# A two-layer streaming encoder step: the gated-linear-attention layer's near score products, and one attention in three, issued between the q and the k products of the next unit

## The chip, the cores and the metric

The kernel runs on one core of a Trainium2 chip. The metric is the device time of one execution in microseconds (us). Five engines each work through their own instructions in order: PE (TensorE: matrix products; its weight loads are shown as PEld), DVE (VectorE), ACT (ScalarE), POOL (GpSimd) and SP (which issues transfers). They wait for one another by semaphores.

## The reference, cut to what matters

The trunk has four blocks: retention, a convolutional feed-forward (FFN), gated linear attention (GLA), a second FFN. Only GLA is touched. Per head it computes, from projections q, k, v and a log gate lg:

```python
def gla_chunk(S, xs):
    q, k, v, lg = xs
    b = jnp.cumsum(lg, axis=1)
    expo = b[:, :, None] - b[:, None, :]          # -inf above the diagonal
    A = jnp.einsum('bihd,bjhd,bijhd->bhij', q, k, jnp.exp(expo))
    intra = jnp.einsum('bhij,bjhe->bihe', A, v)
    cross = jnp.einsum('bihd,bhde->bihe', q * jnp.exp(b), S)
    bL = b[:, -1]
    S_new = jnp.exp(bL)[..., None] * S + jnp.einsum('bjhd,bjhe->bhde', k * jnp.exp(bL[:, None] - b), v)
    return S_new, intra + cross
```

There are 4 heads, keys of 128, values of 256, 1024 prompt rows (one stream) and 32 rows of a running stream.

## The kernel before

GLA walks over 12 units `(h, c)`: head h, and c a third of the 1056 columns (384, 384, 288). A unit has three minor tiles of 128 rows; the third tile of c = 2 is the 32 sample rows. For each unit these steps are written out:

- `project`: `gate` (one product `pz`, on ACT the exponential and logarithm, on DVE the running sum `b`), then `qk_products`: 24 products for q (8 weight tiles, each in high x high, high x low, low x high parts, L133 to L135, tile `pj`) and 24 for k, and `qk_out`, which scales both into `q` (L1097) and `k` (L1099) on DVE.
- `weigh`: seven tiles `x64` to `x1` from `b`, one for each level of the score decomposition (differences on POOL, exponentials on ACT, products with k and q on DVE, L1150 and L1151, two a level), and `e`, `qh`, `ql`, `kd`, `eL`.
- `scores`: the near products into `pb` (diagonal 32x32 blocks L1199, level 16 L1202, levels 8, 4, 2, 1 L1208), then the far products of levels 64 and 32 into `pa` (L1215). They use 32 or 16 columns of the PE array each and are float32, so that each is two matmul records in the trace: 144 near and 24 far in a full unit. Then DVE masks `pb` into `A` (L1220, L1225), and ACT and DVE split `A` and `pa` into `Ah` and `Al` (L1247, L1248).
- `mix`: per minor tile `value` (24 products `pv`, L267 to L269, split into `vh` on ACT and `vl` on DVE) and `attend`: the state product `ouu` (L1338 to L1340), the new state `gS` on DVE (L1343), the output `ou` (L1354 to L1360), whose last product L1360 reads `gSl`, the low part of the state before, made on DVE (L1292) after its high part `gSh` on ACT (L1291). `keys` transposes `kd`; `late` transposes the unit before's output (`pt`, L1410).

The loop overlaps units by the order of the text: in the turn of unit u, the q and k products of the next unit come first, then `store[0]`, the third attention of the unit before u, then the scores of u, then its values and first two attentions. In a unit with c = 2 the third minor tile has no value products, so its second attention comes right after the first and the transposes. A scheduler keeps each engine's order near this text and moves some instructions by its own estimate; the PSUM tiles `pj`, `ou` and `lv` (which holds `pb`, `pa`, `pkt` and `pt`) have two buffers each.

Of the kernel before, what the change touches and what calls it, by code (L numbers as in the profile page):

```python
# [16 lines left out]
P = 128  # L17
# [3 lines left out]
TS = 32  # L21
# [17 lines left out]
def minors(c):  # L39
    c0, n = CM[c]  # L40
    out = []
    o = 0
    while o < n:
        ln = min(128, n - o)
        out.append((o, c0 + o, ln))
        o += ln
    return out
# [3 lines left out]
def trunk_kernel(ctx: ExitStack, tc: tile.TileContext, io):  # L51
    nc = tc.nc
    V, S, G, PE = nc.vector, nc.scalar, nc.gpsimd, nc.tensor
# [1012 lines left out]
    def gla(closers):  # L1066
# [10 lines left out]
        def groups_of(c):  # L1077
            return [(0, 3, P)] if c < 2 else [(0, 2, P), (2, 3, TS)]

        def qk_products(h, c, between=None):  # L1080
            c0, n = CM[c]
            if c == 0:

                wq[h] = weights("w_gqk", h, 0, after=(None, masked[0]))
                wk[h] = weights("w_gqk", h, 1, after=(None, masked[0]))
            pq = t384(pp, "pj", w=512)
            proj(pq[:, :n], wq[h], c0, n)
            if between:
                between()
            pk = t384(pp, "pj", w=512)  # L1090
            proj(pk[:, :n], wk[h], c0, n)
            return pq, pk

        def qk_out(c, ps):
            c0, n = CM[c]
            q = t384(g1, "q")
            V.tensor_tensor(q[:, :n], ps[0][:, :n], R[:, c0:c0 + n], op=ALU.mult)  # L1097
            k = t384(g1, "k")
            V.scalar_tensor_tensor(k[:, :n], ps[1][:, :n], float(GDK ** -0.5), R[:, c0:c0 + n],  # L1099
                                   op0=ALU.mult, op1=ALU.mult)  # L1100
            return q, k
# [14 lines left out]
            V.tensor_tensor_scan(b[:, :n], smask[:, :n], t2[:, :n], 0.0, op0=ALU.mult, op1=ALU.add)  # L1116
            return b

        def project(h, c):
            if (h, c) == (0, 1):  # L1120

                return None, *qk_out(c, qk_products(h, c))
            b = gate(h, c)
            return b, *qk_out(c, qk_products(h, c))

        def weigh(h, c, bqk):
            b, q, k = bqk
# [54 lines left out]
            V.tensor_tensor(kd[:, :n], kd[:, :n], k[:, :n], op=ALU.mult)  # L1182
            return q, k, X, qh, ql, kd, eL

        def scores(h, c, w):
            q, k, X, qh, ql, kd, eL = w
            mins = minors(c)
            groups = groups_of(c)

            full = [(mi, o) for mi, (o, t0, L) in enumerate(mins) if L == P]  # L1190
            F = len(full)

            pb = lv("pb")
            near = pb[:, :3 * TS].rearrange("p (m i) -> p m i", i=TS)
            low = pb[:, 3 * TS:9 * TS].rearrange("p (l m i) -> p l m i", l=4, i=TS // 2)
            for mi, (o, t0, L) in enumerate(mins):
                for a in range(0, L, TS):
                    b = o + a
                    PE.matmul(near[a:a + TS, mi], k[:, b:b + TS], q[:, b:b + TS], start=True, stop=True)  # L1199
                for a in range(0, L, TS):  # L1200
                    b = o + a
                    PE.matmul(near[a:a + TS // 2, mi, TS // 2:], X[16][:, b:b + TS // 2],  # L1202
                              X[16][:, b + TS // 2:b + TS], start=True, stop=True)
            for li, s in enumerate(LOW):
                for mi, (o, t0, L) in enumerate(mins):
                    for a in range(0, L, TS):
                        x = X[s][:, o + a:o + a + TS]
                        PE.matmul(low[a:a + TS, li, mi], x, x.rearrange("p (b t) -> p b t", t=2 * s)[:, :, s:],  # L1208
                                  start=True, stop=True)
            far = lv("pa").rearrange("p (m i) -> p m i", m=3)  # L1210
            for mi, o in full:
                for s, b in ((64, 0), (64, TS), (32, 2 * TS), (32, 0)):
                    c0 = 0 if s == 64 else 2 * TS
                    i0 = o + (2 * TS if s == 64 else b + TS)
                    PE.matmul(far[b:b + TS, mi, c0:c0 + s], X[s][:, o + b:o + b + TS], X[s][:, i0:i0 + s],  # L1215
                              start=True, stop=True)

            A = t384(g1, "A", bufs=1, w=3 * TS).rearrange("p (m i) -> p m i", i=TS)
            for m0, m1, L in groups:
                masked[0] = V.tensor_tensor(  # L1220
                    A[:L, m0:m1], near[:L, m0:m1], dmask[:L].unsqueeze(1).to_broadcast([L, m1 - m0, TS]), op=ALU.mult)
            for li, s in enumerate(LOW):
                for m0, m1, L in groups:
                    M, B = m1 - m0, TS // (2 * s)
                    masked[0] = V.copy_predicated(  # L1225
                        A[:L, m0:m1].rearrange("p m (b t) -> p m b t", t=2 * s)[:, :, :, s:],
                        lmask[:L, li].rearrange("p (b t) -> p b t", t=s).unsqueeze(1).to_broadcast([L, M, B, s]),
                        low[:L, li, m0:m1].rearrange("p m (b t) -> p m b t", t=s))
            if c == 1:
                second_mask[0] = masked[0]  # L1230
            whole[0] = masked[0]

            if len(tri) < 2:
                tri.append([t384(g2, f"{t}{len(tri)}", F32R, 1).rearrange("p (m i) -> p m i", i=P) for t in ("Ah", "Al")])
                for t in tri[-1]:
                    S.activation(t.rearrange("p m i -> p (m i)"), smask, AF.Copy, scale=0.0)
            else:
                tri.reverse()
            Ahv, Alv = tri[-1]
            khv, klv = [t384(g2, t, F32R, 2).rearrange("p (m i) -> p m i", i=P) for t in ("kh", "kl")]  # L1240
            As = g2.tile([P, TS], F32R, tag="As", name=f"As{uid()}", bufs=1) if F < 3 else None
            blocks = [(slice(a, a + TS), slice(a, a + TS), A[a:a + TS, :F]) for a in range(0, P, TS)]
            blocks += [(slice(0, 2 * TS), slice(2 * TS, P), far[:2 * TS, :F, :2 * TS])]
            blocks += [(slice(a, a + TS), slice(a + TS, a + 2 * TS), far[a:a + TS, :F, 2 * TS:3 * TS])
                       for a in (0, 2 * TS)]
            for rows, cols, src in blocks[4:] + blocks[:4]:
                S.copy(Ahv[rows, :F, cols], src)  # L1247
                order(V.tensor_tensor(Alv[rows, :F, cols], src, Ahv[rows, :F, cols].bitcast(F32), op=ALU.subtract),  # L1248
                      whole[0])
            if F < 3:  # L1250
                stack_left(As, A[:TS, F], 1.0)

            def keys():
                pkt = pp.tile([P, 3, P], F32, tag="lv", name=f"pkt{uid()}", bufs=2)
                for mi, (o, t0, L) in enumerate(mins):
                    PE.transpose(pkt[:L, mi], kd[:, o:o + L], ident)
                for m0, m1, L in groups:
                    if L == TS:
                        stack_left(khv[:, m0], pkt[:L, m0], 1.0)
                        continue  # L1260
                    cast[0] = S.copy(khv[:L, m0:m1], pkt[:L, m0:m1])
                    masked[0] = V.tensor_tensor(klv[:L, m0:m1], pkt[:L, m0:m1], khv[:L, m0:m1].bitcast(F32),
                                                op=ALU.subtract)
            return As, Ahv, Alv, qh, ql, khv, klv, eL, keys
# [3 lines left out]
        def mix(h, c, u, late, rows0):  # L1268
# [105 lines left out]
            if c == 0:  # L1374
# [2 lines left out]
                v = g2.tile([TS, GDV], F32, tag="vsum", name=f"vsum{uid()}")  # L1377
                vss[h] = g2.tile([P, GDV], F32R, tag="vhs", name=f"vhs{uid()}")
                stack_sample(vss[h], ps, v, GDV // 2, rc[:TS, 8:9])
            attend(1)  # L1380

            def finish():
                attend(2)
# [22 lines left out]
            def store(lv, room):  # L1406
                for e in range(2):
# [3 lines left out]
                    ot = room()  # L1411
                    S.copy(ot[:, :n], pt.rearrange("p m i -> p (m i)")[:, :n])
                    nc.sync.dma_start(scr_og[2 * h + e, :, c0:c0 + n], ot[:, :n])
            return finish, store, scaled, rows

        def lv(name):
            return pp.tile([P, 3, P], F32, tag="lv", name=f"{name}{uid()}", bufs=2).rearrange("p m t -> p (m t)")
# [30 lines left out]
        def between():  # L1448
            gates_out(0, g00)
            mid.append(mean(1))  # L1450
            early.append(gate(0, 0))
            early.append(gates_in(1))
# [16 lines left out]
        store = None  # L1469
# [3 lines left out]

        for i, u in enumerate(units):
            nxt = units[i + 1] if i + 1 < len(units) else None
            if nxt:
                p = project(*nxt)
            if store:
                store[0]()
            if nxt == (0, 1):  # L1480
                rms_b(2, lv("pr"))
                gates_out(2, gates_in(2))
            sc = scores(*u, w)
            if nxt == (0, 1):
                p = gate(*nxt), *p[1:]
            if store:
                store[2]()
            store = mix(*u, sc, late(store), store and store[3])
            if nxt:
                w = weigh(*nxt, p)  # L1490
# [1069 lines left out]
```

## Time and profile before

| what | value |
|---|---|
| device time, 3 runs | 2743.98 us median, 2743.62 to 2744.26 |
| profiled execution | 2745.33 us |
| its span, first to last instruction | 2743.6 us |
| PE busy | 2711.1 us, 99% of the span |
| DVE busy | 2052.2 us, 75% |
| ACT busy | 1384.6 us, 50% |
| POOL busy | 398.5 us, 15% |
| GLA units | from about 1573 to 1858 us of the span |

Busy times are sums over an engine's instructions. An idle stretch of an engine is shown before the instruction that ended it, with the instruction that released it; "issue" stands where the profile shows nothing that the engine waited for. In the lists of instructions, merged rows carry a count; the start of each row is counted from the span's start.

### The profile page before, as it was taken

To read this page: it belongs to the slowest core of one execution; us is meant where nothing else is said; L and a number is where in the kernel's file an instruction comes from. 1 tells how busy PE (TensorE), PEld (TensorE's weight loads), DVE (VectorE), ACT (ScalarE), POOL (GpSimd) and SP (SyncE) were. 2 spreads that over 40 slices of the span, in tenths; PEclk is the share of its full clock that TensorE was granted. 3 is DMA by queue.
4 is the path that set the end of the run, shared out by engine and by line. 5 is a ranking of instruction groups with operands and counts; after the bars stand their busy time and mean duration, and the time that the engine had idled before them with its cause. 6 is when DMAs were issued, how large, how long until landed. Compare 5 with 4: busy or idle time off the path is not lost. (4 is left out here: it accounts for less than half of the span.)

```text
span 2743.6 us, 55821 instructions
## 1 busy us (share of the span) xinstructions
PE 2711.1 (99%) x22416; PEld 2621.5 (96%) x22416; DVE 2052.2 (75%) x3648; ACT 1384.6 (50%) x2596; POOL 398.5 (15%) x671
## 2 busy tenths in 40 slices
PE   9999999999999999999999999999999999999998
PEld 8999987778999999999999999999999999999998
DVE  7876667776566988888876788875479888888666
ACT  7544355444445544444644467774355444445445
POOL 0000000000112211111211232220132111112113
PEclk9999999999999999999999999999999999999999
DMA  6233455554876244332988511116533433329884
GB/s 244 87 110 110 129 156 158 150 145 122 283 236 225 94 145 138 102 106 87 288 226 215 171 40 54 54 54 209 190 121 102 147 129 104 108 83 296 224 214 122
DMA packets 279444, 410.19 MB, mean 150 GB/s; under 512 B 57168, under 2 KB 209104, under 8 KB 275088
## 3 DMA queue, kind: packets, MB, share of 16 engines
q1 hardware_dynamic: 260384, 347.73, 39.1%
q0 software_dynamic: 18256, 58.35, 9.0%
q8 instruction: 175, 2.87, 0.5%
q14 instruction: 85, 0.70, 0.1%
q10 hardware_dynamic: 544, 0.54, 0.1%
HBM read 264.34 MB, written 142.21 MB: 148 GB/s over the span
## 5 line engine op out<-in xcount | busy, mean ns | idle before, releaser
L419 ACT COPY HR<-pu 128x264 f32<-128x264 f32 x264 | 98.6, 374 | 252.2 <-PE pu L445 246.1
L445 PE MATMUL pu<-XA,wgl 128*128 128x264 f32 x752 | 213.4, 284 | 0.0
L440 PE MATMUL pu<-XA,wgh 128*128 128x264 f32 x752 | 212.8, 283 | 0.4 <-ACT wgh L376 0.4
L444 PE MATMUL pu<-XA,wgh 128*128 128x264 f32 x752 | 212.5, 283 | 0.0
L2142 DVE SCALAR_TENSOR_TENSOR AR<-AR,cw 128x1058 f32<-128x1058 f32 x88 | 116.0, 1320 | 69.9 <-ACT AR L2141 59.2
L2115 DVE TENSOR_TENSOR AR<-HR,pu 128x264 f32<-128x264 f32 (+2 forms) x440 | 144.4, 370 | 4.2 <-ACT HR L419 2.8
L440 PEld LDWEIGHTS pu<-XA,wgh 128*128 128x128 f32 x752 | 141.2, 188 | 0.6 <-ACT wgh L376 0.6
L444 PEld LDWEIGHTS pu<-XA,wgh 128*128 128x128 f32 x752 | 141.2, 188 | 0.0
L445 PEld LDWEIGHTS pu<-XA,wgl 128*128 128x128 f32 x752 | 141.1, 188 | 0.0
L440 PE MATMUL pu<-XA,wsh 128*128 128x264 f32 x464 | 132.5, 286 | 1.6 <-ACT HR L419 0.6
L445 PE MATMUL pu<-XA,wtl 128*128 128x264 f32 x464 | 131.9, 284 | 0.0
L445 PE MATMUL pu<-XA,wsl 128*128 128x264 f32 x464 | 131.8, 284 | 0.0
L440 PE MATMUL pu<-XA,wth 128*128 128x264 f32 x464 | 131.7, 284 | 0.0
L444 PE MATMUL pu<-XA,wsh 128*128 128x264 f32 x464 | 131.4, 283 | 0.0
L444 PE MATMUL pu<-XA,wth 128*128 128x264 f32 x464 | 131.1, 283 | 0.0
L2139 POOL COPY cst<-AR 128x2 f32<-128x2 f32 x88 | 48.4, 551 | 562.6 <-DVE AR L2115 562.6
L2141 ACT ACTIVATE AR<-AR,cw 128x1058 f32<-128x1058 f32 x88 | 111.8, 1273 | 12.5 <-DVE AR L2115 11.2
L2143 DVE SCALAR_TENSOR_TENSOR AR<-AR,cw 128x1058 f32<-128x1058 f32 x88 | 115.8, 1318 | 0.0
L377 DVE TENSOR_TENSOR wtl<-rv,wth 128x1024 fp32r<-128x1024 f32 x58 | 70.9, 1223 | 44.2 <-ACT wth L376 44.2
L376 ACT CAST wgh<-rg 128x1024 fp32r<-128x1024 f32 x58 | 61.0, 1051 | 80.4 <-PE pu L445 77.2
L445 PE MATMUL pu<-XB,wtl 128*128 128x264 f32 x352 | 100.5, 286 | 0.0
L440 PE MATMUL pu<-XB,wth 128*128 128x264 f32 x352 | 99.8, 283 | 0.0
(678 smaller groups left out, 11026.1 us busy)
## 6 DMA issues: line engine op xcount, KB each, us to landing
scr_h<-AR SPq DMA_DIRECT2D x162, 264.0 KB, 2.6
scr_x<-AR POOLq DMA_DIRECT2D x88, 264.0 KB, 6.6
rg<-w_up SPq DMA_DIRECT2D x44, 512.0 KB, 3.6
rv<-w_up SPq DMA_DIRECT2D x44, 512.0 KB, 3.4
raw<-w_ro SPq DMA_DIRECT2D x39, 512.0 KB, 4.8
XA<-scr_h SPq DMA_DIRECT2D x64, 264.0 KB, 4.3
scr_hr<-hl SPq DMA_DIRECT2D x20, 512.0 KB, 3.8
XB<-scr_h SPq DMA_DIRECT2D x34, 264.0 KB, 6.3
```

What stands on the lines that cost most here:

```text
L376: cast[0] = split_cast[0] = S.copy(h, src)
L377: split_end[0] = split_last[0] = V.tensor_tensor(l_, src, h.bitcast(F32), op=ALU.subtract)
L419: ins = S.copy(t, b)
L440: mm = PE.matmul(ps, wh[:, k], x[:, 0, kt], start=m in (1, 2, 4, 5) and kt == 0, stop=False, skip_group_check=True)
L444: PE.matmul(ps, wh[:, k], x[:, 1, kt], start=False, stop=False, skip_group_check=True)
L445: mm = PE.matmul(ps, wl[:, k], x[:, 0, kt], start=False, stop=kt == 3, skip_group_check=True)
L2115: last_put[0] = V.tensor_tensor(u[:, d:d + n], t[:, o:o + n], b[:, o:o + n], op=op)
L2139: G.tensor_copy(cst[:, nt, 0:2], uj[:, TP:TP + 2])
L2141: S.activation(cj, uj[:, 2:T + 4], AF.Identity, scale=cw[:, nt, 2:3], bias=cw[:, nt, 3:4])
L2142: V.scalar_tensor_tensor(cj, uj[:, 1:T + 3], cw[:, nt, 1:2], cj, op0=ALU.mult, op1=ALU.add)
L2143: V.scalar_tensor_tensor(cj, uj[:, 0:T + 2], cw[:, nt, 0:1], cj, op0=ALU.mult, op1=ALU.add)
```

## The change

`scores` is cut in two: `near_scores` (the near products and the masking into `A`) and the rest (far products and the splits). A function `between` is handed down to `qk_products` and called after the q products of the next unit. It issues the second attention of the unit before, if that had been held, and the near scores of the current unit. The second attention is held in the three units with c = 2 that have a successor. The first unit's near scores stay where they were, since `project` returns early for unit (0, 1) without the call; the last unit has no next unit.

```diff
-        def project(h, c):
+        def project(h, c, between=None):
...
-            return b, *qk_out(c, qk_products(h, c))
+            return b, *qk_out(c, qk_products(h, c, between))
...
-        def scores(h, c, w):
-            q, k, X, qh, ql, kd, eL = w
+        def near_scores(h, c, w):
+            q, k, X = w[:3]
...
+            return A
+
+        def scores(h, c, w, A):
+            q, k, X, qh, ql, kd, eL = w
...
-            attend(1)
+            held = c == 2 and (h, c) != units[-1]
+            if not held:
+                attend(1)
+
+            def middle():
+                if held:
+                    attend(1)
...
-            return finish, store, scaled, rows
+            return finish, store, scaled, rows, middle
...
+            A = []
+
+            def between():
+                if store:
+                    store[4]()
+                A.append(near_scores(*u, w))
+
             if nxt:
-                p = project(*nxt)
+                p = project(*nxt, between)
             if store:
                 store[0]()
...
-            sc = scores(*u, w)
+            if not A:
+                between()
+            sc = scores(*u, w, *A)
```

The counts of instructions on every engine stay the same; POOL's and SP's orders, and with them the order of all transfers, stay as they were. PE's, ACT's and DVE's change. Three places follow. In the rows of the change the lines are those of its own text: from 1323 on they stand 5 higher up to 1365 (L1343 is L1338 before, L1348 is L1343, L1365 is L1360), 11 higher later (L1421 is L1410), and L1196, L1199, L1205 are the near products L1199, L1202, L1208. A number behind a name is the buffer's.

PE, at the end of unit (0, 2)'s `mix`: the transposes of the unit before, then the second attention. Before:

```order
L1410 MATMUL pt_18941<-ident,oraw_18431 128x128 x3
L1338 MATMUL ouu_18952<-vh_18911,kh_18811 128x256
L1339 MATMUL ouu_18952<-vh_18911,kl_18812 128x256
L1107 MATMUL pj_19027<-XG_7526 128x384
L1340 MATMUL ouu_18952<-vl_18912,kh_18811 128x256
L133 MATMUL pj_19038<-XA,whi_18653 128x384
L1354 MATMUL ou_18959<-vh_18911,Ah_1039_17975 128x256
```

The same place with the change:

```order
L1421 MATMUL pt_18941<-ident,oraw_18431 128x128 x3
L1107 MATMUL pj_19007<-XG_7526 128x384
L133 MATMUL pj_19018<-XA,whi_18653 128x384
L134 MATMUL pj_19018<-XA,whi_18653 128x384
L135 MATMUL pj_19018<-XA,wlo_18654 128x384
```

The gate product and the q products of the next unit now follow the transposes at once. Behind the last of the 24 q products stands, with the change:

```order
L1343 MATMUL ouu_19047<-vh_18911,kh_18811 128x256
L1344 MATMUL ouu_19047<-vh_18911,kl_18812 128x256
L1345 MATMUL ouu_19047<-vl_18912,kh_18811 128x256
L1359 MATMUL ou_19054<-vh_18911,Ah_1039_17975 128x256
L1360 MATMUL ou_19054<-vh_18911,Al_1040_17976 128x256
L1361 MATMUL ou_19054<-vl_18912,Ah_1039_17975 128x256
L1363 MATMUL ou_19054<-gSh_19043,qh_18626 128x256
L1364 MATMUL ou_19054<-gSh_19043,ql_18627 128x256
L1365 MATMUL ou_19054<-gSl_19044,qh_18626 128x256
L1196 MATMUL pb_19063<-q_18779,k_18781 32x32 x4
```

The nine products of the held attention come as a block, and the near products of unit (1, 0) behind them, ahead of the k products.

DVE, in the same stretch, from the new state of the first attention on. Before:

```order
L1343 SCALAR_TENSOR_TENSOR gS_18923<-gS_18725,eL_18630,ouu_18919 128x256
L1150 TENSOR_TENSOR x_1191_18968<-x_1191_18968,k_18715 128x3x64
L1318 SCALAR_TENSOR_TENSOR vl_18912<-pv_18886,rc,vh_18911 128x256
L1151 TENSOR_TENSOR x_1191_18968<-x_1191_18968,q_18713 128x3x64
L1150 TENSOR_TENSOR x_1192_18974<-x_1192_18974,k_18715 128x6x32
L1343 SCALAR_TENSOR_TENSOR gS_18956<-gS_18923,eL_18630,ouu_18952 128x256
L1151 TENSOR_TENSOR x_1192_18974<-x_1192_18974,q_18713 128x6x32
L1292 TENSOR_TENSOR gSl_18949<-gS_18923,gSh_18948 128x256
```

With the change, the end of the same stretch (between the first row and these stand the fourteen `x` products and `vl`, and nothing else):

```order
L1151 TENSOR_TENSOR x_1192_18984<-x_1192_18984,q_18779 128x192
L1162 TENSOR_TENSOR e_18990<-e_18990,q_18779 128x384
L1111 TENSOR_SCALAR t_1200_19011<-pj_19007,ba 128x384
L1297 TENSOR_TENSOR gSl_19044<-gS_18923,gSh_19043 128x256
L1169 TENSOR_TENSOR ql_18994<-e_18990,qh_18993 128x384
```

`gSl`, which the last product of the held attention reads, moved from the fifth place among the `x` products to behind all of them, `e` and `t`.

PE, in the turn of unit (1, 2), around its near and far products (the other moved units differ in sizes). Before, the whole block stood behind the k products and the third attention of the unit before:

```order
L1360 MATMUL ou_19958<-gSl_19949,qh_19450 128x256
L1199 MATMUL pb_19967<-q_19525,k_19527 32x32 x4
L1202 MATMUL pb_19967<-x_1308_19824 16x16 x4
...
L1208 MATMUL pb_19967<-x_1312_19848 32x16 x9
L1215 MATMUL pa_20022<-x_1306_19812 32x64 x2
```

With the change the near block stands between q and k (`pj_19894`, `pj_19985`), the far block where it was:

```order
L135 MATMUL pj_19894<-XA,wlo_19885 128x384
L1196 MATMUL pb_19919<-q_19604,k_19606 32x32 x4
...
L1205 MATMUL pb_19919<-x_1312_19848 32x16 x9
L133 MATMUL pj_19985<-XA,whi_19890 128x384
...
L1365 MATMUL ou_20024<-gSl_20015,qh_19450 128x256
L1235 MATMUL pa_20033<-x_1306_19812 32x64 x2
```

24 k products and the attention's nine lie between near and far.

More of the change, by code (lines that the diff above doesn't have):

```diff
@@ L1183, in weigh @@
             return q, k, X, qh, ql, kd, eL
-        def scores(h, c, w):
-            q, k, X, qh, ql, kd, eL = w
+        def near_scores(h, c, w):
+            q, k, X = w[:3]
             mins = minors(c)
             groups = groups_of(c)
-            full = [(mi, o) for mi, (o, t0, L) in enumerate(mins) if L == P]
-            F = len(full)
             pb = lv("pb")
@@ L1209, in scores @@
                                   start=True, stop=True)
[L1210 to L1216, printed above, removed]
             A = t384(g1, "A", bufs=1, w=3 * TS).rearrange("p (m i) -> p m i", i=TS)
@@ L1231, in scores @@
             whole[0] = masked[0]
+            return A
+        def scores(h, c, w, A):
+            q, k, X, qh, ql, kd, eL = w
+            mins = minors(c)
+            groups = groups_of(c)
+            full = [(mi, o) for mi, (o, t0, L) in enumerate(mins) if L == P]
+            F = len(full)
+            far = lv("pa").rearrange("p (m i) -> p m i", m=3)
+            for mi, o in full:
+                for s, b in ((64, 0), (64, TS), (32, 2 * TS), (32, 0)):
+                    c0 = 0 if s == 64 else 2 * TS
+                    i0 = o + (2 * TS if s == 64 else b + TS)
+                    PE.matmul(far[b:b + TS, mi, c0:c0 + s], X[s][:, o + b:o + b + TS], X[s][:, i0:i0 + s],
+                              start=True, stop=True)
             if len(tri) < 2:
```

## The prediction

> **What bounds the kernel now.** I read the page first, then PE's waits inside GLA, then the instruction lists around each wait.
>
> ```profile
> span 2743.6 us, 55821 instructions
> ...
> PE 2711.1 (99%) x22416; PEld 2621.5 (96%) x22416; DVE 2052.2 (75%) x3648; ACT 1384.6 (50%) x2596; POOL 398.5 (15%) x671
> ...
> q8 instruction: 175, 2.87, 0.5%
> ```
>
> PE is busy for 99% of the span, so only PE's idle time or its own work can move the end. Its waits from 1573 to 1858 us, the whole of GLA:
>
> ```profile
> PE ouu L1338 <- ACT oraw L1361: 3.1, 3, 1.0
> PE pv L267 <- issue: 2.8, 2, 1.6
> PE pa L1215 <- issue: 1.4, 1, 1.4
> PE ou L1352 <- DVE gS L1343: 0.6, 1, 0.6
> PE pb L1208 <- issue: 0.4, 1, 0.4
> PE pj L1107 <- DVE XG L1438: 0.4, 1, 0.4
> PE ou L1354 <- ACT oraw L1362: 0.3, 1, 0.3
> ```
>
> That is 9.0 us in all. The first row, three waits of 1.0, is the second attention of three c = 2 units, which the change moves. The rows named "issue", 4.6 us, come below. The others lie at GLA's ends and stay. Sums go against the profiled execution's own 2745.33 us (span 2743.6 and 1.7 around it); the median shown, 2743.98, is 1.35 lower.
>
> **The held attention.** PE around the first of the three waits:
>
> ```profile
> 1657.21 0.27 PE L1410 MATMUL pt<-ident,oraw 128*128 128x128 f32 x1
> 1658.51 0.36 PE L1338 MATMUL ouu<-vh,kh 128*128 128x256 f32 x1 [1.03 <-ACT oraw L1361]
> ...
> 1663.86 0.34 PE L134 MATMUL pj<-XA,whi 128*128 128x384 f32 x1
> 1664.04 0.34 PE L135 MATMUL pj<-XA,wlo 128*128 128x384 f32 x1
> 1664.21 0.28 PE L1336 MATMUL ouu<-vhs,kh 96*128 96x256 f32 x1
> 1664.33 0.28 PE L1352 MATMUL ou<-vhs,As 96*32 96x256 f32 x1
> ```
>
> Between about 1657.3, where the transposes leave PE free, and 1664.2 PE does the gate, 24 q products and the nine attention products, and waits: 6.9 us. The starts stand 0.175 us apart for q products and 0.12 for products of 256 columns, so without any wait it would be 0.17 + 24 x 0.175 + 9 x 0.12 = 5.45. The most to be saved is 1.45 a unit, 4.4 for three. But the ninth attention product, due at 1657.3 + 0.17 + 4.2 + 8 x 0.12 = 1662.6, reads `gSl`, which DVE now makes later:
>
> ```profile
> 1657.89 0.48 DVE L1343 SCALAR_TENSOR_TENSOR gS<-gS,eL,ouu 128x256 f32<-128x256 f32 x1
> ...
> 1659.50 0.48 DVE L1343 SCALAR_TENSOR_TENSOR gS<-gS,eL,ouu 128x256 f32<-128x256 f32 x1
> 1659.90 0.35 DVE L1151 TENSOR_TENSOR x<-x,q 128x192 f32<-128x192 f32 x1
> 1660.17 0.42 DVE L1292 TENSOR_TENSOR gSl<-gS,gSh 128x256 fp32r<-128x256 f32 x1
> 1660.50 0.35 DVE L1150 TENSOR_TENSOR x<-x,k 128x192 f32<-128x192 f32 x1
> ...
> 1663.19 0.56 DVE L1162 TENSOR_TENSOR e<-e,q 128x384 f32<-128x384 f32 x1
> 1663.66 0.62 DVE L1111 TENSOR_SCALAR t<-pj,ba 128x384 f32<-128x384 f32 x1
> ```
>
> Without the two moved instructions (0.40 and 0.33 between starts) `e` starts at 1662.46 and `t` at 1662.93; `gSl` behind it, 0.42 long, ends near 1663.9. PE would wait 1.25 us there. DVE may be earlier: with the change most masks and splits of the unit before fall into DVE's idle time ahead of k instead of behind the far products. ACT's casts ahead of the first `gS` keep most of that from showing, and I allow 0.6, so the wait is 0.7 to 1.25. I take 0.95: a unit saves 1.45 - 0.95 = 0.5, three save 1.5 (ends: 0.6, and 4.4 if `gSl` were in time). Behind this wait on PE stand the near products and the k products, so nothing covers it. The values of the third tile need no DVE work there, and the k products need `t` out of `pj`, which is then long done.
>
> **Near products before their levels are ready.** All moved units but the first have `x1` some microseconds ahead. In unit (0, 1) the last q product and the last level product stand so:
>
> ```profile
> 1616.25 0.29 PE L135 MATMUL pj<-XA,wlo 128*128 128x288 f32 x1
> ...
> 1617.49 0.34 DVE L1151 TENSOR_TENSOR x<-x,q 128x192 f32<-128x192 f32 x1
> ```
>
> The near block starts at 1616.45 and comes to level 1 after about 1 us, 1617.45; `x1` ends at 1617.83. Cost 0.4 once (0 to 0.8).
>
> **One more change of array shape per unit.** Near and far were one burst; now there are two, with full-width products between. The price at both ends of a burst:
>
> ```profile
> 1668.77 0.28 PE L1359 MATMUL ou<-gSh,ql 128*32 128x256 f32 x1
> 1668.89 0.28 PE L1360 MATMUL ou<-gSl,qh 128*32 128x256 f32 x1
> 1669.09 0.27 PE L1199 MATMUL pb<-q,k 128*32 128x32 f32 x8
> ...
> 1670.34 0.66 PE L1215 MATMUL pa<-x 128*32 128x32 f32 x22
> 1670.93 0.39 PE L267 MATMUL pv<-whi,XA 128*128 128x256 f32 x1
> 1671.15 0.28 PE L268 MATMUL pv<-wlo,XA 128*128 128x256 f32 x1
> ```
>
> Going in takes 0.20 instead of 0.12, coming out 0.22 instead of 0.12: 0.19 a burst, and ten units get one more: +1.9 us. The ends are 0 and, with a whole product's duration of 0.28 at each side instead of its step, 10 x 2 x 0.16 = 3.2. I stay with the row. [...]
>
> **The waits named "issue".** Each comes in or just behind a burst. Counted in instructions:
>
> ```profile
> 1600.18:1625.14 24.96, 23.37 (x383) 22.39 (x382) 21.70 (x53) 17.85 (x60) 10.83 (x15) 1.00 0.15 45
> 1625.14:1806.77 181.63, 177.10 (x2417) 172.01 (x2417) 147.18 (x449) 130.34 (x438) 51.71 (x82) 0.99 0.17 57
> 1806.77:1832.16 25.39, 24.17 (x382) 23.11 (x383) 18.90 (x63) 18.43 (x65) 7.76 (x12) 1.00 0.21 76
> ```
>
> The stretches run from the end of one such wait to the next; the first two counts are PE's products and weight loads. They sum to 765, 4834 and 765. The page's q8 brought 2.87 MB in 175 packets, 16.4 KB each, and PE's 44832 instructions over 175 are 256. So the waits stand 3, 19 and 3 blocks of 256 apart (768, 4864, 768, the few missing being instructions that only wait): they end where a fetched block begins. The block that ran out began inside the near burst:
>
> ```profile
> 1621.46:1625.14 3.68, 2.10 (x151) 1.00 0.01 4
> 1803.97:1806.77 2.80, 1.36 (x146) 1.00 0.25 61
> 1828.51:1832.16 3.65, 2.44 (x148) 1.00 0.22 86
> 1782.72:1786.65 3.93, 3.93 (x144) 1.00 0.02 4
> ```
>
> Each stretch is one block (the count includes products still running at its start). Three were used up in 2.1, 1.4 and 2.4 us of PE work, and the next block was there only after 2.8 to 3.7; the fourth lasted 3.9 and nobody waited. With the change 33 full-size products (66 instructions with their loads, some 4.1 to 5.3 us at the steps above) lie between near and far, and the near burst starts 58 or 66 instructions earlier. In units (0, 1), (3, 0), (3, 1) the block that begins inside near (now 152, 94 and 160 instructions behind its start, counted back from the waits) then takes in most of these products and lasts 4.8 us or more. All three waits go: 1.59 + 1.45 + 1.22 = 4.3 us. Of the other moved units (1, 0) and (1, 1) come nearest, at 4 and 70: 0 to 0.5 us new. The wait of 0.4 in unit (0, 0) stays. Ends: 0 and -4.7.
>
> [...]
>
> **The clock.** Behind the 1.59 us wait PE ran at half clock:
>
> ```profile
> 1625.00:1626.00 1.00, 0.85 (x5) 0.69 0.00 0
> 1626.00:1627.00 1.00, 1.00 (x6) 0.50 0.07 16
> 1627.00:1628.00 1.00, 1.00 (x7) 0.50 0.00 0
> 1628.00:1629.00 1.00, 1.00 (x7) 0.60 0.00 0
> ```
>
> The third number from the right is the granted clock: 0.31 + 0.5 + 0.5 + 0.4 = 1.7 us lost. It goes with the wait. The profiled execution is 1.35 us above the median, so the timed runs may not hold it at all.
>
> **Sum.** -1.5 (held attention) + 0.4 (`x1`) + 1.9 (array shape) - 4.3 (blocks) - 1.7 (clock) = -5.2 on 2745.33, or 2740.1. On the median it is 2738.8 if the timed runs hold the clock loss, 2740.5 if not; I forecast 2739.8.
>
> **Rivals.** (1) The "issue" waits are not tied to the bursts, or come back in another unit. For it: nothing in the trace names their cause, and only four of twelve bursts have one. Against: the counts of 256. The sum is then -1.5 + 0.4 + 1.9 = +0.8: 2744.8. [...]
>
> (2) `gSl` is in time, since DVE starts its `x` products earlier than I allow: all 4.4 saved, so 2.9 less than my sum, 2736.9 (2735.9 with the clock loss in the timed runs). Against: the DVE list above has no idle row in it. For: DVE has 25% idle over the span, and its masks move into idle time.
>
> (3) Slower: each more change of array shape costs far more than the burst's ends show, because behind the near block the k products start cold. It decides from (5.5 + 4.2)/10 = 1.0 us above the 0.19, 1.2 us a unit; then 2749.5. Against: the far bursts are followed by full-size products already and pay 0.10.
>
> (4) The change does not remove the wait on the held attention, only renames it. That is two thirds of my own first term.
>
> **How the numbers follow.** About 0.2%, 5.5 us, is what a measurement can tell here from no change: 2738.5 to 2749.5 counts as the same. My forecast 0.47, rival 1 0.22, rival 2 0.27, rival 3 0.04. The forecast's own range is 2738.0 to 2742.0; a tenth of it lies below 2738.5. Faster: 0.27 and about 0.03 of the forecast, 0.30; slower 0.04; same 0.66. The range reaches to most of rival 1 and into rival 2: 2736.3 to 2745.0.
>
> **What the changed profile would show.** Right: no "issue" wait at L267 or L1215 in GLA and none above 0.5 us; the clock at 1.00 throughout it; three new waits of PE at L1365 for DVE's `gSl` of 0.7 to 1.25 us, and none at L1343 for ACT; one wait of 0.4 us for DVE's `x1` near 1617; starts 0.20 to 0.25 us apart at both ends of each near block. Wrong: "issue" waits of a microsecond in other units, half clock behind a `gSl` wait, or first k products well above 0.4 us.

## The result, and the profile after

The changed kernel takes 2750.28 us (median of nine runs, 2747.24 to 2754.58) beside 2743.79 of the kernel before (nine runs): a ratio of 1.0023, 95% interval 1.0015 to 1.0032. It is slower, by some 6.5 us. A later series of nine runs gave 2750.64 beside 2743.94, 1.0026 (1.0016 to 1.0036). The forecast was 2739.8, its range ended at 2745.0.

The profiled execution took 2749.51 us. From the page:

```profile
span 2747.7 us, 55843 instructions
...
PE 2716.2 (99%) x22416; PEld 2624.4 (96%) x22416; DVE 2063.5 (75%) x3648; ACT 1382.2 (50%) x2596; POOL 401.0 (15%) x671
```

PE's counts of products and loads are the same, and it is as full as before. I measure GLA from the start of its first gate product to the start of its last output product: 278.97 us before (1578.47 to 1857.44), 284.06 after (1576.84 to 1860.89), and 284.05 in the profile of the later series. So 5.1 us of the loss lie in GLA, and they are the same in two profiles of the changed kernel. The two profiled executions differ by 4.2 us in all and the medians by 6.5; why not both by GLA's 5.1 is open. PE's waits there, in the changed kernel (a row: who waits for whom, us in total, times, the longest):

```profile
PE ouu L1343 <- ACT kh L1266: 3.1, 2, 2.0
PE ou L1365 <- DVE gSl L1297: 1.4, 3, 0.6
PE ouu L1344 <- DVE kl L1267: 1.1, 5, 0.2
PE pb L1205 <- issue: 0.8, 1, 0.8
...
PE pj L135 <- DVE wlo L110: 0.3, 2, 0.2
PE ouu L1343 <- DVE gS L1348: 0.3, 1, 0.3
...
PE pb L1205 <- DVE x L1151: 0.2, 1, 0.2
```

The issue waits at L267 and L1215 are gone, and so are the three for `oraw`. New are the waits at L1343 and L1344: the first attention of a unit waits for its keys, `kh` and `kl`. The largest is in unit (0, 1), 1.97 us up to 1630.46. Behind it PE runs at half clock (the number before the last two is the granted clock):

```profile
1632.00:1633.00 1.00, 1.00 (x9) 0.70 0.00 0
1633.00:1634.00 1.00, 1.00 (x6) 0.50 0.00 0
1634.00:1635.00 1.00, 1.00 (x6) 0.50 0.00 0
1635.00:1636.00 1.00, 1.00 (x8) 0.60 0.28 104
```

0.3 + 0.5 + 0.5 + 0.4 = 1.7 us, as much as behind the issue wait of before: in these profiles the clock loss was not removed but moved.

Why `kh` is late, on DVE in unit (0, 1) before the change:

```profile
1621.03 0.45 DVE L1097 TENSOR_TENSOR q<-pj,R 128x288 f32<-128x288 f32 x1
...
1622.06 0.43 DVE L1099 SCALAR_TENSOR_TENSOR k<-pj,R 128x288 f32<-128x288 f32 x1
1622.40 0.47 DVE L1343 SCALAR_TENSOR_TENSOR gS<-gS,eL,ouu 128x256 f32<-128x256 f32 x1
...
1626.52 0.52 DVE L1248 TENSOR_TENSOR Al<-A,Ah 32x96 fp32r<-32x96 f32 x2
```

and with the change:

```profile
1619.84 0.45 DVE L1097 TENSOR_TENSOR q<-pj,R 128x288 f32<-128x288 f32 x1
...
1621.14 1.05 DVE L1214 COPY_PREDICATED A<-lmask,pb 128x48 f32<-128x48 uint32 x4
1623.64 2.20 DVE L1253 TENSOR_TENSOR Al<-A,Ah 32x96 fp32r<-32x96 f32 x4 [1.45 <-ACT Ah L1252]
1625.87 0.46 DVE L1099 SCALAR_TENSOR_TENSOR k<-pj,R 128x288 f32<-128x288 f32 x1
1626.24 0.47 DVE L1348 SCALAR_TENSOR_TENSOR gS<-gS,eL,ouu 128x256 f32<-128x256 f32 x1
```

With near scores earlier, the scheduler also moved the splits of the near blocks earlier, ahead of `k` and of the third attention's `gS`. The four subtracts `Al` wait 1.45 us for their casts, and those stand on ACT behind six exponentials:

```profile
1621.68 1.76 ACT L1431 ACTIVATE x<-x 128x128 f32<-128x128 f32 x6 [0.25 <-POOL x L1138]
1623.35 1.13 ACT L1252 CAST Ah<-A 32x96 fp32r<-32x96 f32 x4
1626.75 0.41 ACT L1296 CAST gSh<-gS 128x256 fp32r<-128x256 f32 x1 [2.26 <-DVE gS L1348]
...
1629.94 0.47 ACT L1266 CAST kh<-pkt 128x384 fp32r<-128x384 f32 x1
```

So `k` starts 6.03 us behind `q` instead of 1.03, `gS` with it, ACT stands 2.26 us for `gS`, and everything behind `gSh` on ACT, `kh` among it, is late. `kh` needs neither this `k`, which is the next unit's, nor this `gS`: the transposes that it reads had ended at 1625.64. It is late because it stands behind `gSh` in ACT's order. Summed over the twelve units, `k` starts 77.8 us behind `q` instead of 41.8. That sum shows how far DVE's order was pushed and is not the price: in a kernel below that is level with the one before it is still 60.9.

### The profile page after: what moved, and what is told of

It reads as the page before. It is cut to its first block, busy times and chain, and to the rows that moved or that the text cites. A ratio compares the mean times of both kernels' runs of the same rounds, so it can differ in the third digit from the quotient of the medians.

```text
span 2747.7 us, 55843 instructions
## 1 busy us (share of the span) xinstructions
PE 2716.2 (99%) x22416; PEld 2624.4 (96%) x22416; DVE 2063.5 (75%) x3648; ACT 1382.2 (50%) x2596; POOL 401.0 (15%) x671
## 5 line engine op out<-in xcount | busy, mean ns | idle before, releaser
L376 ACT CAST wgh<-rg 128x1024 fp32r<-128x1024 f32 x58 | 60.9, 1051 | 80.4 <-PE pu L445 77.2
```

What stands on the lines that cost most here:

```text
L376: cast[0] = split_cast[0] = S.copy(h, src)
```

## The experiments

There are three theories. Splits: the loss is these early splits. Shape: it is the second burst (run of small products) of each unit. Held attention: it is the wait for `gSl` and its effects. The series ran on four chips; each ratio is against the kernel before on the same chip (medians 2743.8 to 2745.0). The last column is the length of GLA in the one profile of each kernel. Some of these profiles have a stretch of half clock in GLA, which is 1.7 us of it: the change (each time), near alone moved (two stretches), held with early state split, before shifted by 200, and the 278.97 of before.

| kernel | median us | ratio (95%) | GLA in its profile |
|---|---|---|---|
| the change | 2750.28; 2750.64 | 1.0023 (1.0015 to 1.0032); 1.0026 | 284.06; 284.05 |
| late splits | 2744.49 | 0.9998 (0.9989 to 1.0007) | 276.47 |
| late subtracts alone | 2744.19 | 1.0001 (0.9992 to 1.0010) | 276.58 |
| near alone moved | 2751.22 | 1.0024 (1.0015 to 1.0033) | 285.88 |
| held attention alone | 2744.57 | 1.0001 (0.9992 to 1.0010) | 279.21 |
| held, early state split | 2745.36 | 1.0002 (0.9993 to 1.0011) | 280.92 |
| late splits, early state split | 2743.25 | 0.9997 (0.9988 to 1.0005) | 276.90 |
| near alone, late subtracts | 2745.85 | 1.0004 (0.9995 to 1.0013) | 278.26 |
| near and far between, late splits | 2744.10 | 0.9997 (0.9989 to 1.0006) | 276.13 |
| three bursts, late splits | 2745.70 | 1.0005 (0.9996 to 1.0014) | 278.47 |
| before, blocks shifted by 200 | 2750.30 | 1.0022 (1.0013 to 1.0031) | 283.52 |
| before, blocks shifted by 100 | 2745.92 | 1.0006 (0.9997 to 1.0015) | 279.06 |

**Late splits.** In the changed kernel's `scores`:

```diff
-            for rows, cols, src in blocks[4:] + blocks[:4]:
-                S.copy(Ahv[rows, :F, cols], src)
-                order(V.tensor_tensor(Alv..., src, Ahv..., op=ALU.subtract), whole[0])
+            for i, (rows, cols, src) in enumerate(blocks[4:] + blocks[:4]):
+                hi = S.copy(Ahv[rows, :F, cols], src)
+                lo = V.tensor_tensor(Alv..., src, Ahv..., op=ALU.subtract)
+                order(lo, whole[0])
+                if i >= 3 and seen[0] is not None:
+                    order(hi, seen[0])
+                    order(lo, seen[1])
```

`seen` holds the last output copy on ACT and the last `gS` on DVE.

> Near products and the held attention stay where the change puts them on PE. Only the splits of the near blocks move back: their four casts on ACT stand behind the last output copy of the unit before, their four subtracts on DVE behind its last gS, as before the change. Splits theory (the loss comes from these splits standing ahead of k, gS and gSh, so that the next unit's kh and kl come late): PE's waits at attend(0) for kh (3.1 us listed), kl (1.1) and gS (0.3) go, and with them the half clock behind the 1.97 us wait (1.7 us); 2750.3 - 4.5 - 1.7 = 2744.1, between 2742 and 2746. Shape theory (the additional changes of array shape carry the loss): 2749 to 2750, since the bursts are as in the changed kernel. Held-attention theory (the gSl wait and what follows it): 2749 to 2750 too.

2744.49: the whole loss is gone, with both bursts and the held attention as in the change. That rules out the other two theories as its carrier.

**Late subtracts alone.** As above without `order(hi, seen[0])`: ACT's casts stay early.

> As the kernel with the late splits, but only the DVE subtracts of the near blocks stand behind the last gS; the ACT casts stay early, ahead of gSh. If DVE's subtracts ahead of k and gS are the cause: the kh waits are gone as with the late splits, 2744.5, between 2742.5 and 2746.5. If ACT's casts, which wait for the masks and stand ahead of gSh and the output copies, are the cause: 2748 to 2750.5.

2744.19, as with both. DVE in unit (0, 1), and PE's waits in GLA:

```profile
1620.99 0.45 DVE L1097 TENSOR_TENSOR q<-pj,R 128x288 f32<-128x288 f32 x1
...
1623.20 0.45 DVE L1099 SCALAR_TENSOR_TENSOR k<-pj,R 128x288 f32<-128x288 f32 x1
1623.57 0.47 DVE L1350 SCALAR_TENSOR_TENSOR gS<-gS,eL,ouu 128x256 f32<-128x256 f32 x1
1624.80 2.20 DVE L1253 TENSOR_TENSOR Al<-A,Ah 32x96 fp32r<-32x96 f32 x4 [0.76 <-ACT Ah L1252]
```

```profile
PE ouu L1345 <- ACT kh L1268: 0.8, 2, 0.6
PE ou L1367 <- DVE gSl L1299: 0.6, 3, 0.2
...
PE pb L1205 <- issue: 0.5, 1, 0.5
PE ouu L1346 <- DVE kl L1269: 0.5, 2, 0.2
```

The masks (1.05 us) and even the 2.20 us of subtracts are still there, but the latter stand behind `k` and `gS`: `k` starts 2.21 us behind `q`, `kh` makes PE wait 0.8 in all instead of 3.1, `gSl` 0.6 instead of 1.4, and no half clock stands in GLA. The cause is the early place of the four DVE subtracts; the casts, which I had suspected too, cost nothing that these runs can tell. Place and price are not fully apart: beside POOL's differences such a subtract took 0.63 us at the median instead of 0.25 (last section), and 21 of them stand there in the change, 9 here. In unit (0, 1) the price is the same 2.20 us in both kernels, and the wait for `kh` still falls from 1.97 to 0.59, so there it is the place alone.

**Near alone moved.** `held = False` in the changed kernel.

> Only the near products are moved between q and k; the second attention of the c = 2 units stays ahead of the next unit's gate, as before the change. Splits theory: the kh waits at attend(0) of the c = 1 units stay, the three gSl waits (1.9 us with the longer steps) go and the three waits of 1.0 us for oraw (3.8 with the longer steps) come back: 2750.3 + 1.9 = 2752, between 2750 and 2754. Shape theory: the same, 2752. Held-attention theory: 2743 to 2745.

2751.22. The moved near scores carry the loss by themselves. The waits for `kh` are the longest again, and both long ones (1.94 and 1.01 us) have half clock behind them:

```profile
PE ouu L1343 <- ACT kh L1266: 3.6, 4, 1.9
PE ouu L1344 <- DVE kl L1267: 0.9, 4, 0.2
PE ouu L1343 <- DVE gS L1348: 0.7, 3, 0.3
```

```profile
1636.00:1638.00 2.00, 2.00 (x11) 0.50 0.00 0
...
1824.00:1826.00 2.00, 2.00 (x11) 0.50 0.24 86
```

The three waits of 1.0 us for `oraw` did not come back: at the three second attentions PE waits 0.17, 0.16 and 0.54. The 3.8 us that I had set for them was wrong.

**Held attention alone.** `near_scores` is called right ahead of `scores`; `between` only issues the held attention.

> Only the second attention of the c = 2 units is moved between the q and the k products; near and far stay one burst, as before the change. Splits theory and shape theory: no mask or split stands ahead of k and there is one burst a unit, so the kh waits are not there, the issue waits of 1.59, 1.45 and 1.22 us are, and the held attention saves 3.8 - 1.9 = 1.9 us: 2743.8 - 1.9 = 2741.9, between 2741 and 2743.5. Held-attention theory: 2747 to 2751.

2744.57, a miss of both numbers: nothing gained. The three waits of 1.0 only change their name:

```profile
PE ou L1365 <- DVE gSl L1297: 3.0, 3, 1.0
PE pv L267 <- issue: 2.8, 2, 1.4
```

**Held, early state split.** As the last one, and

```diff
             if not held:
                 attend(1)
+            else:
+                ready.append(split_state(state[h], ""))
```

with `attend(1)` taking the pair from `ready`.

> Only the second attention of the c = 2 units is held, near and far are one burst as before the change, and gSh and gSl are issued ahead of the next unit's level products. If gSl's place behind DVE's list is all that turns the held wait into a renamed one: the three waits of 1.0 us (1.15 with the longer steps) go, 2744.6 - 3.4 = 2741.1, between 2739.5 and 2743. If the next link is as late (the level products, e or t pushed behind gSl): 2744 to 2745.

2745.36, 0.4 above the range of the second alternative, whose mechanism came true. `gSl` is in time, and the same wait stands one link on, at the first q product, which needs the buffer that DVE's `t` reads:

```profile
PE pj L133 <- DVE t L1111: 2.9, 3, 1.0
PE pv L267 <- issue: 2.5, 2, 1.3
PE pa L1235 <- issue: 2.4, 1, 2.4
```

At the end of a c = 2 unit DVE as a whole is 1.0 us late, whichever of its results PE asks for. The issue wait at `pa` also grew from 1.45 to 2.4.

**Late splits and early state split** together:

> As the kernel with the late splits, and in the held attention the split of the state into gSh and gSl is issued right after the first attention, ahead of the level products of the next unit, instead of between q and k. Splits theory: the kh waits go as with the late splits, and the three gSl waits (1.4 us listed, 1.9 with the longer steps) go too: 2744.1 - 1.6 = 2742.5, between 2740 and 2744.5. Shape theory: 2748 to 2749, only the gSl waits go. Held-attention theory: the whole loss goes with the gSl waits, 2740 to 2743, but then the late splits alone show 2749 to 2750.

2743.25, within what was expected and within the uncertainty of the kernel before. It is the lowest median of all, and not a proven gain. Its profile lists a granted clock of 0.95 outside the half-clock stretches; the median step of a value product is 0.117 us there and 0.119 in the late splits, so nothing in GLA was slower for it.

**Near alone, late subtracts.**

> As the kernel whose DVE subtracts stand behind the last gS, but with the second attention of the c = 2 units back ahead of the next unit's gate. Ledger of the traces (with DVE freed the held attention's waits shrink from 3.8 to 1.1 us): 2744.2 + 2.7 = 2746.9, between 2745.5 and 2748.5. If the held attention only hands its wait on: 2744.2, between 2743 and 2745.5.

2745.85, at the lower end of the ledger's range. GLA is 278.26 long beside 276.58 with the held attention: with the subtracts late, holding saves 1.7 us by the profiles, not 2.7. The subtracts are worth some 5.5 us in this kernel too: the ratio falls from 1.0024 to 1.0004.

**Near and far between, late splits.** The far products move into `near_scores` too, and all splits get the two `order` lines.

> Near and far are both between the q and the k products, in one burst, the second attention is held, and all splits of A (near and far blocks) stand behind the last gS and output copy. One change of array shape per unit less than with the late splits alone: at 0.25 us a unit 2744.5 - 2.5 = 2742. If waits for fetched instruction blocks come back with the longer burst, up to three of 1.5 us: 2746. If the shape costs nothing: 2744.5.

2744.10, between the alternatives. The one burst does save a change of shape a unit, and brings issue waits back:

```profile
PE pa L1227 <- issue: 2.2, 1, 2.2
PE pj L133 <- issue: 1.7, 1, 1.7
```

GLA is 0.3 us shorter than with late splits alone: some 2.9 saved in shape (0.29 a unit, below), the waits for `kh` and `kl` gone (0.6), some 3.4 lost in issue waits and 0.5 in a new wait for `t`; the rest is in the longer steps behind waits.

**Three bursts, late splits.** The near blocks and level 16 go ahead of the q products, the lower levels between q and k.

> As the kernel with the late splits, but the near burst is cut in two: the near blocks (and level 16) ahead of the q products, the lower levels between q and k, so a unit has three bursts. Shape price as read from the trace, 0.25 us a unit: 2744.5 + 2.5 = 2747. Shape theory at 0.5 us a unit (what the whole loss would need): 2749.5. Shape free: 2744.5.

2745.70; GLA 2.0 us longer than with late splits. New waits of 1.2 (`ot`) and 0.3 more for `x` are in it, and 1.7 of others (`gSl`, `kl`, `kh`, `wlo`) are gone. Nothing near the 5 us more that the shape theory needs.

**Before, blocks shifted.** In the kernel before, unit (0, 0) issues its last far product 50 more times, or its first near product 25 more times:

```diff
+            if (h, c) == (0, 0):
+                for _ in range(25):
+                    PE.matmul(near[:TS, 0], k[:, :TS], q[:, :TS], start=True, stop=True)
```

> The kernel before the change, with the last far product of unit (0, 0) issued 50 more times (the same values again), so that 100 more PE instructions stand ahead of everything behind it and the blocks of 256 begin elsewhere. Block theory (a block that begins some 24 to 100 instructions behind a burst's start is used up before the next one is there): the issue waits of 1.59, 1.45 and 1.22 us go, one new wait of about 1.5 us comes in unit (2, 1) near 1763 us, whose block then begins 76 behind the burst's start, and the 50 products cost 0.4: 2744.3 - 4.3 + 1.5 + 0.4 = 2741.9, and up to 1.7 less where the half clock behind the first wait had been in the timed runs: 2740 to 2742.5. If the waits hang on something else (a DMA, a place in the loop): they stay where they are, 2744.7.

> The kernel before the change, with the first near product of unit (0, 0) issued 25 more times ahead of the near block. An f32 product of this kind is four PE instructions, as the kernel with 50 more far products showed (200 more recorded), so this shifts the blocks by 100; DVE and ACT keep their order. Block theory: the waits of 1.59, 1.45 and 1.22 us go; the block now begins 76 instructions behind the burst's start in unit (2, 1), a wait of about 1.7 us near 1763, and 102 behind it in unit (1, 0), 0 to 0.8 near 1673. With 0.4 for the products: 2744.6 - 4.3 + 1.7 + 0.4 + 0.4 = 2742.8, and up to 1.7 less with the half clock: 2740.5 to 2744. If the waits do not hang on the count: they stay, 2745.

The first has an error of mine in it: such a float32 product is four PE instructions, so 50 of them shift by 200, not by 100 (the trace holds 45144 PE records instead of 44944). By 200 the blocks begin 60 and 92 behind the burst's start in units (1, 1) and (3, 0), and in the dangerous stretch in no other unit with three full tiles (in (2, 2), whose burst is shorter, one begins at 90, and nobody waits); the two waits of its trace stand in just these units, at 1701.07 and 1815.71:

```profile
PE pvs L279 <- DVE vl L1322: 2.9, 1, 2.9
PE pa L1215 <- issue: 1.9, 1, 1.9
PE pv L267 <- issue: 1.3, 1, 1.3
```

Its time tells nothing of blocks: the 50 products took 3.4 us instead of 0.4, and the longer burst made the scheduler reorder DVE and ACT in unit (0, 0), which goes with the wait of 2.9 us for `vl` and the half clock behind it. The second, shifted by 100 with DVE's and ACT's orders kept, has:

```profile
PE pa L1218 <- issue: 1.9, 1, 1.9
PE ouu L1342 <- DVE kl L1265: 1.1, 1, 1.1
...
PE pv L269 <- issue: 0.5, 1, 0.5
PE pj L135 <- DVE wlo L110: 0.4, 1, 0.4
```

The 1.9 us stand in unit (2, 1) at 1764.74 and the 0.5 in unit (1, 0) at 1674.09, both as written down ahead of the run; the three old waits are gone. The block theory holds in place and size. Yet the time is 2745.92, 3 us above what was expected. 1.2 of it is that the 25 products took 1.6 us, not 0.4. Most of the rest is a wait that had been under the old one: in unit (0, 1), where the issue wait and the half clock had held PE back for 3.3 us, PE now comes 1.1 us too early to `kl` and behind that 0.4 too early to `wlo`.

**The change again.**

> The changed kernel as it is, on the chip of the other experiments, so that their differences to it rest on the same chip: every theory expects the first result, 2750.3, between 2748.5 and 2752.

2750.64, as expected, though on a fourth chip and not on that of the other runs. Its half clock stands behind another wait than in the first profile: at 1818 us, behind a `kh` wait of 1.05, while the one of 1.99 at 1630.5 has none.

## Why the prediction was wrong, step by step

The sum, each wait taken with the longer step that goes with it (the time from one product's start to the next, less the usual step of that pair):

| term | predicted | in the profiles |
|---|---|---|
| held attention | -1.5 | -1.9 (3.8 to 1.9) |
| `x1` in unit (0, 1) | +0.4 | +0.4 |
| array shape | +1.9 | +2.9 |
| fetched blocks | -4.3 | -4.4 (5.4 to 1.0) |
| clock | -1.7 | 0, moved |
| `kh`, `kl`, `gS` at the first attention | none | +6.6 |
| `wlo` at the q products | none | +0.7 |
| sum | -5.2 | +4.3 of the 5.1 measured; 0.8 not assigned |

**The step that failed** is a sentence in the held attention's part: "with the change most masks and splits of the unit before fall into DVE's idle time ahead of k instead of behind the far products". I used it as a reason why `gSl` might come earlier. It was read as free time. But the splits do not fill idle time, they wait in it: for casts on ACT, which wait for exponentials, which wait for POOL. And behind them on DVE stand `k` and `gS`. I followed what is queued behind the waiting instruction only on PE, and in my list of signs wrote "none at L1343 for ACT", where the 3.1 us came. In the sum this step has no term at all; it measured 6.6 us, and the 1.7 us of clock that were to go stand behind one of its waits. The late subtracts show that this single place on DVE is worth the whole 6 us: with them the time is level with the kernel before.

**Fetched blocks.** Right in place and size. In the kernel before, the issue waits of 0.43, 1.59, 1.45 and 1.22 us end at PE records 24001, 24770, 29634 and 30401 (products, weight loads and waits counted from 0), in the changed kernel the one of 0.82 at record 24001: 193 or 194 modulo 256 each time. Each of the five ends 1.2 to 1.5 us after a packet of 16.4 KB of the queue q8 has landed (at 1623.79 us for the wait that ends at 1625.15). The kernel shifted by 100 has 1.9 us at a place that was computed ahead. What was wrong is the use of the number: I took a wait that goes for time that is won. In unit (0, 1) it had covered DVE's late `kl`, as the kernel shifted by 100 shows without any near product moved. That fits the late splits, which stay level with the kernel before although nearly all issue waits are gone.

**Clock.** The loss followed the longest waits to new places, but not by their length alone. It stands behind waits of 1.01, 1.05, 1.59, 1.94, 1.97, 2.4 and 2.9 us, and not behind others of 1.08, 1.9, 1.99 and 2.2. The clock record in the traces says more. Each stretch of half clock in GLA lasts 3.41 us, and where a trace has several they start a whole number of such lengths apart: 187.74 us or 55 lengths in near alone, 1109.33 us or 325 in the kernel before and in the change, where the later one stands at the span's end. Laid on that grid, the traces that hold such a stretch show this: 3.41 us of GLA with 1.59 us or more of idle PE were followed by half clock each time (five cases, 1.59 in the kernel before and 1.71 in the change among them), with 1.22 us (the kernel before) or less never, with 1.24 to 1.58 us two times of nine (in near alone, behind 1.24, and in the change again). The wait of 1.99 us was cut by the grid into 1.30 and 0.69 and had none. So in these traces where a wait falls decides in part whether it costs 1.7 us or nothing, and what decides in the nine cases stays open.

**Array shape.** It is 0.29 us a unit instead of 0.19. In unit (1, 1), where the usual step is 0.13:

```profile
1688.05 0.29 PE L135 MATMUL pj<-XA,wlo 128*128 128x288 f32 x1
1688.28 0.27 PE L1196 MATMUL pb<-q,k 128*32 128x32 f32 x8
...
1689.67 0.40 PE L133 MATMUL pj<-XA,whi 128*128 128x288 f32 x1
1689.90 0.29 PE L134 MATMUL pj<-XA,whi 128*128 128x288 f32 x1
```

The step into near and the step behind the first k product are each 0.10 longer, near the 0.08 and 0.10 that I had read at the ends of the old burst. Left out was a third place, from near's last small product to the first k product: 0.11, where before the step from near to far took 0.015.

**Held attention.** The sum of -1.5 is near -1.9 by accident. The wait of 0.95 that I took is the 0.99 of the held attention alone, where nothing is gained (rival 4), since DVE is 1.0 us late there. In the change the three waits are only 0.20, 0.59 and 0.63. Holding gains 1.7 once the subtracts stand late.

**The rivals.** Rival 3 named 2749.5, nearly the time measured, for another reason: it needed 1.2 us of shape a unit, and the trace has 0.29. That is luck. No rival had DVE's queue ahead of `k` as its mechanism. The case of the other sign was looked for on PE, the full engine, where the change moves things on purpose, not on DVE, where the scheduler moved things as a consequence.

## What to carry to other kernels

When a block of work is issued earlier, look up where its follow-up on the other engines lands, and price what is queued behind it there: here a follow-up that waited 1.45 us at the head of DVE's queue delayed everything behind it (`k` 6.03 us behind `q` instead of 1.03), on an engine that is 25% idle. A wait that vanishes is won only if the next releaser is early by as much; ask for each what arrives last when it is gone. And after such a move, pin the follow-up back by hand before judging the move itself.

## What the runs showed of the hardware

In unit (0, 1) the same subtract `Al` of 32x96 takes 0.61 to 0.63 us while POOL works on its differences (three of the four that take 2.20; the fourth, begun at 1625.58, takes 0.26), and 0.26 (0.52 for two) in the kernel before, where POOL is nearly done:

```profile
1621.03 4.41 POOL L1138 TENSOR_TENSOR x<-b 128x256 f32<-128x256 f32 x7 [8.02 <-DVE b L1116]
```

That is POOL in the changed kernel, to 1625.44; in the kernel before it worked to 1626.58, when the `Al` at 1626.52 quoted above began:

```profile
1622.22 4.36 POOL L1138 TENSOR_TENSOR x<-b 128x256 f32<-128x256 f32 x7 [8.03 <-DVE b L1116]
```

So the early place also raised the price of the work. Over all of GLA 21 such subtracts stand for the most part beside these differences in the changed kernel, with a median of 0.63 us (0.61 to 0.88); the 28 of the kernel before stand clear of them, but for up to 0.26 of the time of four, with 0.25. Not all of DVE's work was longer there: `k`, which reads `pj` and `R`, took 0.45 for 288 columns with POOL at its differences (late subtracts alone) and 0.46 without (the change, units (1, 2), (2, 2) and (3, 2)). Why `Al` was, no run shows.

Repeating one small product into the same place was not cheap: the 25 repeats took 1.6 us and the 50 of the other kernel 3.4, 0.03 us a record, where the near products, which change their place in `pb`, step 0.007 (the median, in the kernel before and in the change).
